# Four of eight block pairs by seven products, in alternation, in a hybrid decoder layer

## The chip, the core and the metric

The kernel runs on one core of a Trainium2 chip. The metric is the device time of one execution in microseconds (us); lower is better. The core's engines are TensorE (PE in the profile, its weight loads PEld), VectorE (DVE), ScalarE (ACT), GpSimd (POOL) and SyncE (SP). Here SP does nothing but issue the weight loads.

## What is computed

One decoder layer over 256 tokens of width 2048, all in float32: an input projection to 10240 columns, block attention over 8 heads and a short gated convolution side by side, their outputs gated by sigmoids, a mixing projection, cross-attention to 256 memory tokens, a squared-ReLU MLP of width 8192, and a final RMS norm. Cut to the lines that matter here:

```python
h = rms_norm(x, norm_mix)
q, k, v, cx, cb, cc, ga, gc = split_in_proj(h @ w_in)      # ga, gc: 2048 columns each
merged = sigmoid(ga) * y_attn + sigmoid(gc) * y_conv
x = x + merged @ w_mix_out
...
u = relu(rms_norm(x, norm_mlp) @ w_up)                     # 8192 columns
return rms_norm(x + (u * u) @ w_down, norm_final)
```

The two pieces that the change touches are `h @ w_in` for the gate columns, and `(u * u) @ w_down`.

## The kernel before

Every float32 product is made of three fp32r matmuls. A weight block arrives from memory as `raw`; ScalarE writes its rounded part `whi` (L71) and VectorE the remainder `wlo = raw - whi` (L72), 128 x 1024 at a time. The activations are split in the same way once. A product is then hi x hi + hi x lo + lo x hi, three 128x512 matmuls into one PSUM bank (lines 171 to 173 in the functions below).

Most projections go through `tok_group` or `feat_group`. The gate columns (three groups of 1024 columns: the second gate of the first half, and both gates of the second half) and the down projection go through `pair_group`, eleven calls in all. For the down projection the 8192 hidden features are taken in four rounds `g` of 2048. A round first makes its 2048 features by `feat_group` on `w_up` (four times 512), then calls `pair_group` twice (`jp` 0 and 1), each time for 1024 of the 2048 output columns.

`pair_group` works on 2 x 2 blocks: two halves of 128 tokens, two column blocks of 512, and eight pairs of 128-row contraction blocks. A pair is done in one of two ways:

- **direct**: four outputs of two products each, so 8 products or 24 matmuls. Of the weights it needs two splits of 128 x 1024 on each of ACT and DVE.
- **seven** (Strassen's scheme in Winograd's form): 7 products or 21 matmuls. DVE first makes four sums of weight blocks, `tsum` (L139 to L142, 128 x 512 each), which are split too. In all DVE has four sums, one split `olo` of 128 x 512 (L132) and three splits `wlo` of 128 x 1024. The sums of activations that it needs are made once for all calls, by `act_sums` into `hS` and `uS`.

The products of all pairs gather in eight PSUM banks, all that there are: six from the pool `mm` (`acc`) and two from `aux` (`aps`). Direct pairs add into four of them (numbers 2, 3, 4, 8), seven pairs into seven (1 to 7). When the last seven pair of a call is done, banks 1, 5, 6 and 7 are final, and ACT (L208) and DVE (L209 to L212) combine them into four blocks `p1, u4, u3, v`. When the last direct pair is done, banks 2, 3, 4 and 8 are final as well, and the call's consumer adds them: for the down projection `add_down` on DVE, L609 (the combined block into the residual `tok`) and L610 (the bank into `tok`), four of each per call; for the gates L466 on DVE and a sigmoid on ACT. The next call needs the same eight banks.

The order of the pairs in a call is a table, `MIXED` for the gates and `MIXED2` for the down projection, both with the same entries (pair, by seven or not). The order of instructions on each engine is not that of the code: a scheduler with a model of the chip's time sets it when the program is built. What limits how far one engine can run ahead are the buffers: four `raw`, five `whi`/`wlo`, two `tsum`, one `ohi`/`olo`. A load into a `raw` buffer is issued by SP, in order, as soon as ACT and DVE have read what was in it.

In the last call the final output block is halved (`fine`), and `last_sum` and `store` form the final norm. GpSimd helps with products by the norm's gain for the first half of the columns (L638).

## Time and profile before

| | |
|---|---|
| time, median of 3 runs | 1453.58 us (1453.27 to 1454.04) |
| the profiled execution | 1452.71 us, span of its instructions 1450.9 us |
| PE busy, share of the span | 1433.7 us, 99% |
| PEld (weight loads) | 1200.4 us, 83% |
| DVE | 1025.6 us, 71% |
| ACT | 752.2 us, 52% |
| POOL | 14.4 us, 1% |
| share of 16 DMA engines, mean rate | q1 59.7%, 195 GB/s |

The profile shows one execution. The span runs from its first to its last instruction. Busy time of PE is the union of matmul durations, which overlap each other, so 99% does not say that no time is lost between them; the distance between the starts of two matmuls does. The same holds of DVE: a duration in its rows reaches some hundredths of a microsecond into the next instruction, and the distance between two starts is what the instruction costs in a queue. Behind a row in brackets stands how long the engine sat idle before it, and what ended that.

### The profile page before, as it was taken

Reading aid. Unit: us, or ns where it says so; the run is one execution under the profiler, and the core shown is the slowest. Engines: PE = TensorE matmul, PEld = TensorE weight load, DVE = VectorE, ACT = ScalarE, POOL = GpSimd, SP = SyncE. Lnnn points to the kernel's source line nnn. Section 1 sums busy time; section 2 is a strip of 40 time slices with the busy share of each in tenths; the row PEclk is TensorE's granted clock in tenths of the full one; section 3 lists DMA queues with packets and bytes.
Section 4 is the critical chain, followed back from the end, with each engine's and each line's share of the span. In section 5 each row is a group of like instructions: output and inputs, shape, how many; then the busy total and the mean of one; then the engine's idle time right before and its main releaser. Section 6 shows DMA issues by size and latency. Waiting matters only on the chain.

```text
span 1450.9 us, 18458 instructions
## 1 busy us (share of the span) xinstructions
PE 1433.7 (99%) x6923; PEld 1200.4 (83%) x6923; DVE 1025.6 (71%) x1346; ACT 752.2 (52%) x999; POOL 14.4 (1%) x20
## 2 busy tenths in 40 slices
PE   8999999999999999999999999999999999999997
PEld 6888888888878888888888888888888888888875
DVE  6645555667679756654477689668896689866897
ACT  7644444445445545564565455445554555444553
POOL 0000000000000000000000000000000000000010
PEclk9999999999999999999999999999999999999999
DMA  9766555565656767755556566665665556655554
GB/s 320 231 192 185 169 176 172 170 193 189 198 169 196 233 221 266 237 186 186 162 174 183 181 194 211 192 196 170 199 217 190 188 161 212 219 192 183 179 176 145
DMA packets 122938, 283.39 MB, mean 195 GB/s; under 512 B 8928, under 2 KB 9696, under 8 KB 122464
## 3 DMA queue, kind: packets, MB, share of 16 engines
q1 hardware_dynamic: 119088, 273.58, 59.7%
q10 hardware_dynamic: 3760, 8.63, 1.8%
q8 instruction: 54, 0.88, 0.3%
q14 instruction: 36, 0.29, 0.1%
HBM read 280.08 MB, written 2.10 MB: 194 GB/s over the span
## 4 chain that ended last, share of the span: by engine, by line
PE 95%; DVE 2%; DMA 1%; ACT 0%; issue 0%; POOL 0%; SPq 0%; POOLq 0%; DVEq 0%; ACTq 0%
PE acc L83 15%; PE acc L108 13%; PE acc L110 13%; PE acc L109 13%; PE acc L84 8%; PE acc L172 6%; PE acc L173 6%; PE acc L171 6%; PE aps L171 4%; PE aps L172 4%; PE aps L173 4%; DMA raw<-in_w_in_dram 1%; PE acc L87 1%; PE aps L262 1%; DVE wlo L72 1%; PE acc L86 1%
## 5 line engine op out<-in xcount | busy, mean ns | idle before, releaser
L72 DVE TENSOR_TENSOR wlo<-raw,whi 128x1024 fp32r<-128x1024 f32 (+1 forms) x483 | 581.0, 1213 | 307.6 <-ACT whi L71 301.9
L71 ACT ACTIVATE whi<-raw 128x1024 fp32r<-128x1024 f32 (+1 forms) x483 | 500.5, 1050 | 401.2 <-PE acc L110 134.2
L83 PE MATMUL acc<-S,whi 128*128 128x512 f32 x960 | 341.6, 398 | 0.0
L108 PE MATMUL acc<-whi,S 128*128 128x512 f32 x816 | 315.5, 389 | 5.0 <-ACT whi L71 5.0
L110 PE MATMUL acc<-whi,S 128*128 128x512 f32 x816 | 317.3, 389 | 0.0
L109 PE MATMUL acc<-wlo,S 128*128 128x512 f32 x816 | 316.7, 388 | 0.0
L84 PE MATMUL acc<-S,wlo 128*128 128x256 f32 x960 | 269.6, 281 | 0.0
L83 PEld LDWEIGHTS acc<-S,whi 128*128 128x128 f32 x960 | 180.2, 188 | 41.1
L84 PEld LDWEIGHTS acc<-S,wlo 128*128 128x128 f32 x960 | 181.3, 189 | 3.1
L108 PEld LDWEIGHTS acc<-whi,S 128*128 128x128 f32 x816 | 153.6, 189 | 35.4 <-ACT whi L71 5.7
L109 PEld LDWEIGHTS acc<-wlo,S 128*128 128x128 f32 x816 | 153.7, 188 | 30.4
L110 PEld LDWEIGHTS acc<-whi,S 128*128 128x128 f32 x816 | 153.6, 188 | 30.2
L71 ACT ACTIVATE whi<-tsum 128x1024 fp32r<-128x1024 f32 x66 | 69.3, 1058 | 92.0 <-DVE tsum L142 41.8
L172 PE MATMUL acc<-wlo,S 128*128 128x512 f32 x255 | 99.6, 391 | 0.0
L173 PE MATMUL acc<-whi,S 128*128 128x512 f32 x255 | 99.1, 389 | 0.0
L172 PE MATMUL aps<-wlo,S 128*128 128x512 f32 (+1 forms) x253 | 98.3, 388 | 0.0
L173 PE MATMUL aps<-whi,S 128*128 128x512 f32 (+1 forms) x253 | 98.1, 388 | 0.0
L171 PE MATMUL aps<-whi,S 128*128 128x512 f32 (+1 forms) x253 | 95.4, 389 | 0.7 <-DVE tok L610 0.7
L171 PE MATMUL acc<-whi,S 128*128 128x512 f32 x255 | 92.5, 389 | 0.0
L72 DVE TENSOR_TENSOR wlo<-tsum,whi 128x1024 fp32r<-128x1024 f32 x66 | 79.1, 1219 | 15.1 <-ACT whi L71 14.2
L172 PEld LDWEIGHTS acc<-wlo,S 128*128 128x128 f32 x255 | 47.9, 188 | 10.9 <-DVE wlo L72 1.0
L171 PEld LDWEIGHTS aps<-whi,S 128*128 128x128 f32 x253 | 47.5, 188 | 11.3 <-DVE tok L610 1.1
(171 smaller groups left out, 1352.2 us busy)
## 6 DMA issues: line engine op xcount, KB each, us to landing
raw<-in_w_in_dram SPq DMA_DIRECT2D x156, 512.0 KB, 4.4
raw<-in_w_up_dram SPq DMA_DIRECT2D x128, 512.0 KB, 3.9
raw<-in_w_down_dram SPq DMA_DIRECT2D x128, 512.0 KB, 4.7
raw<-in_w_mix_out_dram SPq DMA_DIRECT2D x32, 512.0 KB, 5.0
raw<-in_w_attn_out_dram SPq DMA_DIRECT2D x16, 512.0 KB, 4.9
raw<-in_w_conv_out_dram SPq DMA_DIRECT2D x16, 512.0 KB, 4.5
raw<-in_wkv_x_dram SPq DMA_DIRECT2D x16, 512.0 KB, 4.4
raw<-in_wq_x_dram SPq DMA_DIRECT2D x8, 512.0 KB, 4.0
```

Source lines behind the costliest of these rows:

```text
L71: last_split[0] = nc.scalar.activation(hi[:, k:k + step, :], raw[:, k:k + step, :], AF.Copy)
L72: nc.vector.tensor_sub(lo[:, k:k + step, :], raw[:, k:k + step, :], hi[:, k:k + step, :].bitcast(F32))
L83: nc.tensor.matmul(ps, a, xs(k, 2), start=(k == 0), stop=False)
L84: nc.tensor.matmul(ps[:, S:], c, xs(k, 0), start=False, stop=False)
L86: nc.tensor.matmul(ps[:, S:], c, xs(k, 0), start=False, stop=False)
L87: nc.tensor.matmul(ps, a, xs(k, 2), start=(k == 0), stop=True)
L108: nc.tensor.matmul(ps, xh, wh, start=(k == 0), stop=False)
L109: nc.tensor.matmul(ps, xh, wl, start=False, stop=False)
L110: nc.tensor.matmul(ps, xl, wh, start=False, stop=(k == nk - 1))
L171: nc.tensor.matmul(ps, ah, bh, start=first, stop=False)
L172: nc.tensor.matmul(ps, ah, bl, start=False, stop=False)
L173: nc.tensor.matmul(ps, al, bh, start=False, stop=final)
```

## The change

The number of pairs that go by seven products rises from three to four, and the table of pairs becomes a strict alternation of seven and direct: pairs 0 to 3 by seven, 4 to 7 direct. Before, the three seven pairs alternated with three direct ones and two more direct pairs stood at the end. `NSEVEN` also sets how many activation sums are made for the gates; for the down projection `uS` and the condition in `ev_u` are widened to match.

```diff
-NSEVEN = 3
+NSEVEN = 4
...
-    MIXED = [(0, True), (3, False), (1, True), (4, False), (2, True), (5, False), (6, False), (7, False)]
-    MIXED2 = [(0, True), (3, False), (1, True), (4, False), (2, True), (5, False), (6, False), (7, False)]
+    MIXED = [(0, True), (4, False), (1, True), (5, False), (2, True), (6, False), (3, True), (7, False)]
+    MIXED2 = [(0, True), (4, False), (1, True), (5, False), (2, True), (6, False), (3, True), (7, False)]
...
-        uS = big.tile([P, 3, 2, 512], F32R, name="SS")
+        uS = big.tile([P, 4, 2, 512], F32R, name="SS")
...
-                    if k < 6:
+                    if k < 8:
                         act_sums(uS, k // 2, t)
```

Since a scheduler sets the order, the rows below show what it made of the table at three places. Numbers behind a name tell buffers apart.

DVE before, where the first call of round 0 ends and the second begins: from the last sums of the next call's first seven pair to the first split (`wlo_7236`) of that call's first direct pair.

```order
L141 TENSOR_TENSOR tsum_7182<-raw_7179,tsum_7181 128x512
L72 TENSOR_TENSOR wlo_7192<-raw_7179,whi_7191 128x1024
L142 TENSOR_TENSOR tsum_7182<-raw_7179,tsum_7182 128x512
L72 TENSOR_TENSOR wlo_7196<-tsum_7181,whi_7195 128x1024
L72 TENSOR_TENSOR wlo_7200<-tsum_7182,whi_7199 128x1024
L139 TENSOR_TENSOR tsum_7272<-raw_7268 128x512
L610 SCALAR_TENSOR_TENSOR tok_4397<-acc_6862,q3_6020,tok_4397 128x512
L140 TENSOR_TENSOR tsum_7272<-raw_7270,raw_7268 128x512
L610 SCALAR_TENSOR_TENSOR tok_4397<-acc_6866,q3_6020,tok_4397 128x512
L72 TENSOR_TENSOR wlo_7236<-raw_7231,whi_7235 128x1024
```

The row ahead of these is `wlo_7134`, the last split of the first call; L209 to L212 and all four L609 stand further ahead, among the splits of the direct pairs at the call's end.

DVE now, at the same place, up to the split `wlo_7297` that answers to `wlo_7236`. Ahead of these rows stand `wlo_7195` (the last split of the first call), an L609 and the split `olo_7249` (L132).

```order
L72 TENSOR_TENSOR wlo_7253<-raw_7240,whi_7252 128x1024
L209 TENSOR_TENSOR blk_7222<-acc_6928,blk_7222 128x512
L72 TENSOR_TENSOR wlo_7257<-tsum_7242,whi_7256 128x1024
L72 TENSOR_TENSOR wlo_7261<-tsum_7243,whi_7260 128x1024
L210 TENSOR_TENSOR blk_7223<-acc_6924,blk_7222 128x512
L211 TENSOR_TENSOR blk_7223<-acc_6920,blk_7222 128x512
L139 TENSOR_TENSOR tsum_7333<-raw_7329 128x512
L610 SCALAR_TENSOR_TENSOR tok_4440<-acc_6912,q3_6063,tok_4440 128x512
L140 TENSOR_TENSOR tsum_7333<-raw_7331,raw_7329 128x512
L212 TENSOR_TENSOR blk_7224<-acc_6920,blk_7223 128x512
L609 SCALAR_TENSOR_TENSOR tok_4440<-blk_7223,q3_6063,tok_4440 128x512 x2
L72 TENSOR_TENSOR wlo_7297<-raw_7292,whi_7296 128x1024
```

L209 to L212 and three of the four L609 have moved from ahead of the last split of the first call to between it and the first direct split of the second. The other three rounds read the same.

PE before, in the same stretch, up to the first matmul that needs `wlo_7236`:

```order
L171 MATMUL acc_7207<-whi_7235,S2_6029 128x512
L171 MATMUL acc_7211<-whi_7235,S2_6029 128x512
L171 MATMUL acc_7219<-whi_7195,SS_6030 128x512
L172 MATMUL acc_7219<-wlo_7196,SS_6030 128x512
L173 MATMUL acc_7219<-whi_7195,SS_6030 128x512
L171 MATMUL acc_7223<-whi_7199,SS_6030 128x512
L172 MATMUL acc_7223<-wlo_7200,SS_6030 128x512
L173 MATMUL acc_7223<-whi_7199,SS_6030 128x512
L171 MATMUL acc_7203<-ohi_7278,S2_6029 128x512
L172 MATMUL acc_7207<-wlo_7236,S2_6029 128x512
```

PE now, up to the first matmul that needs `wlo_7297`:

```order
L171 MATMUL acc_7276<-whi_7256,SS_6073 128x512
L172 MATMUL acc_7276<-wlo_7257,SS_6073 128x512
L173 MATMUL acc_7276<-whi_7256,SS_6073 128x512
L171 MATMUL acc_7264<-ohi_7339,S2_6072 128x512
L171 MATMUL acc_7280<-whi_7256,SS_6073 128x512
L172 MATMUL acc_7280<-wlo_7257,SS_6073 128x512
L173 MATMUL acc_7280<-whi_7256,SS_6073 128x512
L171 MATMUL acc_7276<-whi_7347,SS_6073 128x512
L171 MATMUL acc_7280<-whi_7347,SS_6073 128x512
L172 MATMUL acc_7268<-wlo_7297,S2_6072 128x512
```

From the first matmul on the last split of the first call (`wlo_7195`) to this last row there are 30 matmuls; ohi_7339 and whi_7347, of the call's second seven pair, are pulled ahead of the direct pair that precedes it.

DVE at the end of the program, from the last split on: before,

```order
L72 TENSOR_TENSOR wlo_11970<-raw_11963,whi_11969 128x1024
L610 SCALAR_TENSOR_TENSOR tok_4397<-acc_11698,q3_6020,tok_4397 128x512
L610 SCALAR_TENSOR_TENSOR tok_4397<-acc_11702,q3_6020,tok_4397 128x512
L638 TENSOR_TENSOR tok_4397<-tok_4397,S3_6022 128x512
L642 TENSOR_REDUCE pre0_6025<-ssf_6024 128x1
L610 SCALAR_TENSOR_TENSOR tok_4397<-aps_11718,q3_6020,tok_4397 128x512
```

and now:

```order
L72 TENSOR_TENSOR wlo_12129<-raw_12122,whi_12128 128x1024
L209 TENSOR_TENSOR blk_12163<-acc_11862,blk_12163 128x512
L210 TENSOR_TENSOR blk_12164<-acc_11858,blk_12163 128x512
L211 TENSOR_TENSOR blk_12164<-acc_11854,blk_12163 128x512
L212 TENSOR_TENSOR blk_12165<-acc_11854,blk_12164 128x512
L609 SCALAR_TENSOR_TENSOR tok_4440<-blk_12164,q3_6063,tok_4440 128x512 x2
L609 SCALAR_TENSOR_TENSOR tok_4440<-blk_12165,q3_6063,tok_4440 128x256
L610 SCALAR_TENSOR_TENSOR tok_4440<-acc_11846,q3_6063,tok_4440 128x512
```

L209 to L212 and three L609 now stand behind the last split; before, they stood ahead of it.

## Rows read from the trace of the kernel before

**Rows 1.** The page's first part: busy us, share of the span, instructions.

```profile
PE 1433.7 (99%) x6923; PEld 1200.4 (83%) x6923; DVE 1025.6 (71%) x1346; ACT 752.2 (52%) x999; POOL 14.4 (1%) x20
```

**Rows 2.** The page's chain that ended last, by engine.

```profile
PE 95%; DVE 2%; DMA 1%; ACT 0%; issue 0%; POOL 0%; SPq 0%; POOLq 0%; DVEq 0%; ACTq 0%
```

**Rows 3.** Waits of PE: who waited for whom, us in total, times, longest.

```profile
PE acc L108 <- ACT whi L71: 5.0, 2, 4.6
PE aps L171 <- DVE tok L610: 0.7, 1, 0.7
```

**Rows 4.** Timeline of PE: start, us, instruction; a first gate call.

```profile
337.94 0.39 PE L171 MATMUL acc<-whi,SS 128*128 128x512 f32 x1
338.16 0.39 PE L172 MATMUL acc<-wlo,SS 128*128 128x512 f32 x1
338.39 0.39 PE L173 MATMUL acc<-whi,SS 128*128 128x512 f32 x1
338.62 0.39 PE L172 MATMUL acc<-wlo,S 128*128 128x512 f32 x1
```

**Rows 5.** Groups of DVE instructions by line: count, then busy us, mean ns.

```profile
L132 DVE TENSOR_TENSOR olo<-raw,ohi 128x512 fp32r<-128x512 f32 x33 | 23.7, 717 | 0.0
L209 DVE TENSOR_TENSOR blk<-acc,blk 128x512 f32<-128x512 f32 x11 | 7.5, 682 | 0.0
```

**Rows 6.** Busy time by stretch; round 0's two down calls, then round 1's `w_up`.

```profile
833.42:916.90 83.48, 83.48 (x366) 68.35 (x365) 75.35 (x90) 43.99 (x49) 0.00 (x0) 1.00 0.64 203
930.00:1005.00 75.00, 75.00 (x427) 65.00 (x425) 51.58 (x73) 36.01 (x50) 0.00 (x0) 1.00 0.60 190
```

**Rows 7.** Timeline of DVE between round 0's two down calls.

```profile
865.52 0.74 DVE L609 SCALAR_TENSOR_TENSOR tok<-blk,q,tok 128x512 f32<-128x512 f32 x1
866.18 0.68 DVE L139 TENSOR_TENSOR tsum<-raw 128x512 f32<-128x512 f32 x1
866.78 0.74 DVE L609 SCALAR_TENSOR_TENSOR tok<-blk,q,tok 128x512 f32<-128x512 f32 x1
...
869.31 1.22 DVE L72 TENSOR_TENSOR wlo<-raw,whi 128x1024 fp32r<-128x1024 f32 x1
870.45 0.69 DVE L141 TENSOR_TENSOR tsum<-raw,tsum 128x512 f32<-128x512 f32 x1
...
877.67 0.69 DVE L140 TENSOR_TENSOR tsum<-raw 128x512 f32<-128x512 f32 x1 [1.00 <-DMA raw<-in_w_down_dram]
878.28 0.75 DVE L610 SCALAR_TENSOR_TENSOR tok<-acc,q,tok 128x512 f32<-128x512 f32 x1
878.94 1.22 DVE L72 TENSOR_TENSOR wlo<-raw,whi 128x1024 fp32r<-128x1024 f32 x1
```

**Rows 8.** Timeline of PE: first matmuls on wlo_7134 and on wlo_7236.

```profile
873.02 0.39 PE L172 MATMUL acc<-wlo,S 128*128 128x512 f32 x1
...
880.21 0.50 PE L172 MATMUL acc<-wlo,S 128*128 128x512 f32 x1
```

**Rows 9.** Timelines, DVE's last split of a direct pair and PE's first use.

```profile
849.81 1.22 DVE L72 TENSOR_TENSOR wlo<-raw,whi 128x1024 fp32r<-128x1024 f32 x1
852.37 0.39 PE L172 MATMUL acc<-wlo,S 128*128 128x512 f32 x1
...
897.38 2.35 DVE L72 TENSOR_TENSOR wlo<-raw,whi 128x1024 fp32r<-128x1024 f32 x2
902.86 0.39 PE L172 MATMUL acc<-wlo,S 128*128 128x512 f32 x1
```

**Rows 10.** Timeline of DVE, and loads of `w_down`: count, KB, us to landing.

```profile
845.73 0.69 DVE L139 TENSOR_TENSOR tsum<-raw 128x512 f32<-128x512 f32 x1 [3.19 <-DMA raw<-in_w_down_dram]
raw<-in_w_down_dram SPq DMA_DIRECT2D x128, 512.0 KB, 4.7
```

**Rows 11.** Timelines of PE, DVE and POOL at the program's end.

```profile
1440.45 0.28 PE L173 MATMUL acc<-whi,S 128*128 128x256 f32 x1
...
1440.40 0.47 DVE L610 SCALAR_TENSOR_TENSOR tok<-aps,q,tok 128x256 f32<-128x256 f32 x1
1440.80 0.15 DVE L617 TENSOR_TENSOR rf<-ssf,pre 128x1 f32<-128x1 f32 x1
...
1442.26 0.47 DVE L610 SCALAR_TENSOR_TENSOR tok<-acc,q,tok 128x256 f32<-128x256 f32 x1
1442.65 0.74 DVE L627 SCALAR_TENSOR_TENSOR tok<-tok,rf,S 128x512 f32<-128x512 f32 x1
...
1444.40 0.57 POOL L618 TENSOR_TENSOR rf<-rf,mhalf 128x1 f32<-128x1 f32 x1 [0.69 <-DVE rf L617]
```

## The prediction

> **What bounds the kernel now.** I read the page's first part, then the chain, PE's waits, and then the stretches of the two down calls one by one. PE is busy 99% of the span [rows 1] and makes 95% of the chain that ended last [rows 2], and in the whole program it is seen to wait for others only a few times, once for 4.6 us and otherwise for 0.7 us or less [rows 3]. So TensorE sets the time. What a matmul costs is not its duration of 0.39 us but the step to the next start: 338.16 to 338.39 to 338.62 is 0.227 us, with no gap where seven pair and direct pair meet [rows 4]. The granted clock is 1.00, the 2.4 GHz level, throughout the down calls [rows 6].
>
> DVE is idle 29% of the span, but that is an average. In the 83.48 us of round 0's two down calls it works 75.35 us, 90%; in the `w_up` stage between, 51.58 of 75 us [rows 6]. The reserve in the stage that the change loads is 8.1 us, and it is not free: DVE sits waiting there for weights, once for 3.19 us [rows 10]. And PE's cover is thin at one place. Where the first call passes into the second, DVE ends the split `wlo_7236` at 878.94 + 1.22 = 880.16 [rows 7] and PE uses it at 880.21 [rows 8]: a lead of 0.05 us. Nothing stalled in this execution, but nothing was left.
>
> **What the change removes.** One `olo` split comes with each seven pair and one L209 with each call, 33 and 11 [rows 5]: three seven pairs in eleven calls. A fourth turns 24 matmuls into 21 in each call, 33 matmuls in all, at 0.227 us each [rows 4]: **-7.5 us** on the engine that is the chain. Of TensorE the Trainium skill (TensorE: Matmul & The Clock Gate, Back-to-back issue gap) gives some 131 ns as the sustained distance at 512 columns; the trace shows 227, and the measurement decides. By the page's figure, as an estimate, the saving would be 4.3 us and the forecast 3.2 us later.
>
> **What it adds to DVE.** In a full queue a 128x512 sum or split costs 0.60 us (866.18 to 866.78), an L609 or L610 0.66 (865.52 to 866.18), a 128x1024 split 1.14 (869.31 to 870.45) [rows 7]. A seven pair is then 5 x 0.60 + 3 x 1.14 = 6.42 us of DVE, a direct pair 2.28: **+4.1 us per call**. A down call's DVE work, with 4 x 0.60 for L209 to L212 and 8 x 0.66 for L609 and L610, goes from 3 x 6.42 + 5 x 2.28 + 7.7 = 38.4 us to 42.5; PE's goes from 183 x 0.227 = 41.5 to 180 x 0.227 = 40.9. Before, DVE had 3 us to spare per call; now it is 1.6 us over. The Trainium skill (Perfetto Trace Analysis, Identifying the Most-Contended Engine) says to judge TensorE by its weight loads rather than its matmuls, and to relieve the engine that is fullest; in these two calls weight loads take 68.35 of 83.48 us, 82%, against DVE's 90%, so by that rule the change helps the wrong engine.
>
> ACT gains 1.5 splits of 1024 a call and is busy 43.99 of 83.48 us [rows 6], so it covers them. The fourth activation sum (four small sums and a split) falls into `w_up`, where DVE is idle a third of the time, and into the start for the gates, where it is likewise hidden; if not, some 2 us five times, which I put into no term since nothing waits on it for tens of microseconds. Loads are the same in number and size.
>
> **Where it lands: between the two down calls.** Before, the call ended with three direct pairs, 3 x 24 x 0.227 = 16 us of PE for 6.8 us of DVE. In that slack DVE did L209 to L212 and the L609. Now the last seven pair is second to last, so its banks are final one pair, 5.4 us, before the end, and this work moves behind the last split. I check the reckoning on before: from the end of `wlo_7134` (869.31 + 1.22 = 870.53) to that of `wlo_7236` (880.16) DVE took 9.63 us, 8.28 of work by the prices above and the rest around the 1.00 us wait for a load [rows 7]. PE used the two at 873.02 and 880.21, 7.19 us apart [rows 8]. The lead was 2.49 us, and 2.49 + 7.19 - 9.63 = 0.05: it closes.
>
> Now the same sum for the changed order. From the end of `wlo_7195` to that of `wlo_7297` DVE has 14 instructions: four splits of 1024 (4.56), three L609 and one L610 (2.64), seven of 0.60 (L132, L209 to L212, L139, L140; 4.20), together 11.4 us. PE has 30 matmuls there, 6.8 us. DVE's lead at `wlo_7195` I take from five direct pairs that follow a seven pair in round 0, from 851.03 to 852.37 = 1.34 us (the first of them) to 899.73 to 902.86 = 3.13 us (the last) [rows 9]; the others are 1.86, 1.43 and 2.10, and the mean is 2.0. So PE waits 11.4 - 6.8 - 2.0 = 2.6 us. The next two splits are late as well: `wlo_7301` comes 1.74 us later (L141, split) where PE has 6 matmuls, 1.36 us: 0.4 more; `wlo_7344` 2.4 us later (L132, L609, split) for 8 matmuls, 1.8 us: 0.6 more. A wait for a load is likely too, since a seven pair holds its `raw` buffers longer and a load lands 4.7 us after its issue [rows 10]: 0 to the 1.0 us of before [rows 7], I take 0.5. That is **4.1 us per round**, 16.2 in four. Bounds: the lead of 3.13 and no load wait, 2.4 a round, 9.6; the lead of 1.34 and 1.0, 5.2 a round, 20.9. After that the alternation gives DVE 8.7 us of work for 10.2 us of PE in each two pairs, so it regains a lead and I count nothing until the end of the second call, where the evacuation meets `w_up` with its idle DVE.
>
> Between the two gate calls of the second half the same happens, with L466 (0.60 each) in place of L609 and L610: 16 instructions, 4 x 1.14 + 12 x 0.60 = 11.8 us against 37 matmuls, 8.4 us, less the lead of 2.0: **1.4 us** (0.2 to 3.0). The first gate call is followed by `tok_group`, which asks little of DVE: nothing.
>
> **The end of the program.** Before, the last L610 starts at 1442.26, 1.69 us after PE's last matmul gave way (1440.45 + 0.12) [rows 11]. Now DVE has after its last split four combinations (2.4), three L609 (1.7), three full and one half L610 (2.4), the halves and the L638 (2.4): 8.9 us until that last L610, while PE needs 2.3 us from that split's first use to its end. With a lead of 2.0 it starts 4.6 us after PE, 2.9 later than before. Both L617 now stand behind it, with L627 and L631 for the first half behind them (before, L617 came at 1440.80 and L627 at 1442.65, under cover [rows 11]): 0.7 more. **+3.6 us** (1.5 to 6).
>
> **The sum** against the profiled execution: 1452.71 - 7.5 + 16.2 + 1.4 + 3.6 = 1466.4 us. The runs' median is 0.87 us above that execution, so **1467 us**; the bounds of the terms give +3.8 to +22.4, 1457 to 1476.
>
> **Rivals.** A: the cover holds. If DVE enters each boundary with some 5 us more lead than I take, all 7.5 us come through: 1446 us. For it speaks that PE hardly ever waited, and the lead in front of some splits is above 4 us; against it, 0.05 us at the place itself, and more DVE work than PE work in a call. It ends faster. Chance 0.12. B: DVE becomes the bound but drops its idle time. The two calls of a round then take 75.35 + 8.28 = 83.6 us instead of 83.48, the gates keep their 2 us, and only the end is paid: +2.0, 1455.6 us, no change. For it: a late engine makes its loads early for the one that waits. Against: loads are issued when DVE has read the buffer, so a late DVE makes late loads. Chance 0.14. C: DVE keeps its 8.1 us of idle time per round, because the four `raw` buffers and not the boundary set the pace: 83.6 + 8.1 - 83.5 = 8.2 us a round, 33 in all, with the end and the gates' saving 1488 us. It decides from the point where each alternation, not just each boundary, shows DVE waiting for loads. Chance 0.09. That the change does not do what it says is ruled out by the order: the fourth sum and split are there, and 21 matmuls where 24 were.
>
> **Chances.** The forecast has 0.65. About 0.2%, 2.9 us, is what a measurement of this kernel can tell from no change. Faster is A, 0.12; the same is B, 0.14; slower is the forecast and C, 0.74. The range runs from 1449 us, between A and B, to 1478, above the bounds and short of C.
>
> **What would show it.** PE waiting for DVE (L72, or L610 through a bank) by 2 to 5 us in each round some 40 us after its down calls begin, with DVE above 95% busy in the two calls; gaps in PE's starts nowhere else but between the gates and at the end; PE's count down by 33. If those gaps are missing, the lead was the wrong term. If DVE waits for loads in each pair, it is C. If the last L610 starts within 2 us of PE's end, the end was.

## The result and the profile after

The changed kernel is slower: 1487.97 us (1486.0 to 1491.39) against 1453.42 (1453.22 to 1454.04) for the kernel before on the same chip, a ratio of 1.0234 [1.0215, 1.0252], the brackets holding the 95% interval. Of each run below the time, its range and its ratio to the kernel before, measured beside it, stand in the same form. The sign of the forecast was right; its size was not: 1467 us was forecast, with a range to 1478.

The page of the changed kernel gives TensorE's and DVE's busy time, then the chain of work that ended last, by engine and by line, and then the group of the first weight sum, L139: the busy time of the group, the mean duration of one, and the idle time in front of them with what ended it.

```profile
PE 1440.1 (97%) x6890; PEld 1195.3 (80%) x6890; DVE 1078.8 (73%) x1439; ACT 772.3 (52%) x1026; POOL 19.3 (1%) x20
...
PE 69%; DVE 13%; DMA 12%; issue 3%; ACT 1%; POOL 0%; SPq 0%; POOLq 0%; DVEq 0%; ACTq 0%
...
L139 DVE TENSOR_TENSOR tsum<-raw 128x512 f32<-128x512 f32 x44 | 31.5, 716 | 53.0 <-DMA raw<-in_w_down_dram 41.1
```

In the chain before, PE made 95%, DVE 2% and DMA 1% [rows 2]; now DMA has 12%. The 33 matmuls are gone (6923 to 6890), but DVE waits 53.0 us in front of L139, 41.1 of them for a load of `w_down`. Before, that was 23.8 and 16.8 us for 33 of them.

PE's waits, longest first in total (us, times, longest), were one of 4.6 us and little else before [rows 3]. Now:

```profile
PE acc L172 <- DVE wlo L72: 9.1, 11, 2.1
PE acc L171 <- DVE blk L210: 5.4, 4, 1.4
PE acc L171 <- DVE tok L610: 5.3, 4, 1.5
PE acc L171 <- ACT whi L71: 4.8, 4, 1.2
PE acc L108 <- ACT whi L71: 4.6, 1, 4.6
PE acc L171 <- ACT ohi L131: 1.8, 3, 0.9
```

Four at L210, four at L610 and four at `whi`: one for each round. The four rounds' down calls, as stretches of the span (duration, then busy time of PE, PEld, DVE, ACT and POOL with the count of instructions, then granted clock, DMA share, GB/s):

```profile
833.99:924.25 90.26, 84.03 (x360) 66.77 (x359) 79.44 (x96) 47.16 (x53) 0.00 (x0) 1.00 0.57 185
1014.90:1105.70 90.80, 84.33 (x361) 66.69 (x360) 79.40 (x96) 47.02 (x53) 0.00 (x0) 1.00 0.59 185
1196.30:1288.30 92.00, 85.47 (x361) 68.01 (x360) 79.56 (x96) 47.09 (x53) 0.00 (x0) 0.98 0.57 182
1378.90:1472.00 93.10, 86.57 (x367) 68.85 (x365) 81.37 (x97) 46.36 (x58) 6.09 (x4) 0.96 0.46 147
```

Round 0 took 83.48 us before [rows 6]. The table shows where the 35.5 us between the two spans (1450.9 and 1486.4) went. A stretch runs from the start of its first matmul to that of its last.

| stretch | before | after | difference |
|---|---|---|---|
| down calls, round 0 | 83.50 | 90.27 | +6.8 |
| round 1 | 83.14 | 90.79 | +7.7 |
| round 2 | 83.11 | 91.92 | +8.8 |
| round 3 | 85.27 | 93.05 | +7.8 |
| the three gate calls | 41.47 + 85.37 | 41.37 + 84.40 | -1.1 |
| last matmul's start to the end of the span | 10.5 | 14.5 | +4.0 |
| start to the first gate call | 332.9 | 334.5 | +1.6 |

The last line is not the change: that start lies between 332.7 and 335.4 us in the runs below, whatever the table of pairs. The loss is in the down calls, and in each round alike. A round of the changed kernel is 360 matmuls, 359 steps of 0.227 us or 81.5 us; the rest, 8.8 us in round 0, is lost time.

The longer end is seen in the start of PE's last matmul, of the last L610 and of the last L617 (before: 1440.45, 1442.26 and, under cover, 1440.80 [rows 11]):

```profile
1471.95 0.28 PE L173 MATMUL acc<-whi,S 128*128 128x256 f32 x1
...
1475.89 0.48 DVE L610 SCALAR_TENSOR_TENSOR tok<-acc,q,tok 128x256 f32<-128x256 f32 x1
...
1477.01 0.16 DVE L617 TENSOR_TENSOR rf<-ssf,pre 128x1 f32<-128x1 f32 x1 [0.51 <-ACT junk L636]
```

DVE's instructions in round 0 (start, duration, in brackets the idle time ahead and what ended it). The four L139 are the first sums of the last two seven pairs of the first call and of the first two of the second; the two L72 are the splits of the first call's last direct pair:

```profile
845.03 0.69 DVE L139 TENSOR_TENSOR tsum<-raw 128x512 f32<-128x512 f32 x1 [2.39 <-DMA raw<-in_w_down_dram]
...
850.25 0.69 DVE L132 TENSOR_TENSOR olo<-raw,ohi 128x512 fp32r<-128x512 f32 x1
...
857.85 0.69 DVE L139 TENSOR_TENSOR tsum<-raw 128x512 f32<-128x512 f32 x1 [2.91 <-DMA raw<-in_w_down_dram]
...
861.93 0.69 DVE L132 TENSOR_TENSOR olo<-raw,ohi 128x512 fp32r<-128x512 f32 x1
...
868.19 0.69 DVE L139 TENSOR_TENSOR tsum<-raw 128x512 f32<-128x512 f32 x1 [1.56 <-DMA raw<-in_w_down_dram]
869.36 0.69 DVE L140 TENSOR_TENSOR tsum<-raw 128x512 f32<-128x512 f32 x1 [0.48 <-DMA raw<-in_w_down_dram]
...
870.57 1.22 DVE L72 TENSOR_TENSOR wlo<-raw,whi 128x1024 fp32r<-128x1024 f32 x1
...
872.31 1.22 DVE L72 TENSOR_TENSOR wlo<-raw,whi 128x1024 fp32r<-128x1024 f32 x1
...
880.78 0.69 DVE L139 TENSOR_TENSOR tsum<-raw 128x512 f32<-128x512 f32 x1 [0.79 <-DMA raw<-in_w_down_dram]
```

Each of the four L139 waits for its load. In strict alternation a seven pair's weights come into the two buffers that the seven pair before it has used. That pair holds the first of them from L139 to the end of L132 (845.03 to 850.94, and 857.85 to 862.62), and only then does the reload begin: 6.9 us until the next L139, then 5.6. Three turns take 880.78 - 845.03 = 35.75 us, 11.9 each, while PE needs 45 matmuls, 10.2 us, for a seven and a direct pair. DVE falls behind by 1.7 us a turn until PE waits. Before, the last seven pair of round 0's first call waited so too (3.19 us [rows 10]), but three direct pairs followed it, and the next L139, at 866.18 [rows 7], waited for nothing.

PE's stall comes where the prediction put it, at the passage, and it meets an engine without a lead:

```profile
871.84 0.50 PE L172 MATMUL acc<-wlo,S 128*128 128x512 f32 x1 [1.20 <-DVE wlo L72]
...
874.27 0.39 PE L172 MATMUL acc<-wlo,S 128*128 128x512 f32 x1
```

The first row uses the first split of the last direct pair, which DVE ends at 870.57 + 1.22 = 871.79, behind two sums that have waited 1.56 and 0.48 us for loads; it starts 1.36 us later than a step of 0.227 would have it. The second row uses the call's last split. Five more such delays, of 0.4 to 1.5 us, follow at 879.45, 882.19, 885.55, 889.99 and 894.77; the six make 7.2 us of the 8.8. Of the signs that the prediction named, the waits at the passage came and PE's count is down by 33; DVE above 95% busy did not come. It is 88% busy in the two calls, 79.44 of 90.26 us.

### The profile page after: what moved, and what is told of

It reads as the page before. It is cut to its first block, busy times and chain, and to the rows that moved or that the text cites. A ratio compares the mean times of both kernels' runs of the same rounds, so it can differ in the third digit from the quotient of the medians.

```text
span 1486.4 us, 18542 instructions
## 1 busy us (share of the span) xinstructions
PE 1440.1 (97%) x6890; PEld 1195.3 (80%) x6890; DVE 1078.8 (73%) x1439; ACT 772.3 (52%) x1026; POOL 19.3 (1%) x20
## 4 chain that ended last, share of the span: by engine, by line
PE 69%; DVE 13%; DMA 12%; issue 3%; ACT 1%; POOL 0%; SPq 0%; POOLq 0%; DVEq 0%; ACTq 0%
PE acc L83 14%; PE acc L108 11%; PE acc L110 11%; PE acc L109 11%; DMA raw<-in_w_down_dram 8%; PE acc L84 7%; DVE wlo L72 6%; DMA raw<-in_w_in_dram 4%; PE acc L172 3%; PE acc L173 2%; PE acc L171 2%; PE aps L173 1%; PE aps L172 1%; PE aps L171 1%; DVE tsum L141 1%
## 5 line engine op out<-in xcount | busy, mean ns | idle before, releaser
L72 DVE TENSOR_TENSOR wlo<-raw,whi 128x1024 fp32r<-128x1024 f32 (+1 forms) x472 | 568.6, 1215 | 264.5 <-ACT whi L71 258.4
L108 PE MATMUL acc<-whi,S 128*128 128x512 f32 x816 | 315.2, 390 | 4.7 <-ACT whi L71 4.6
L110 PE MATMUL acc<-whi,S 128*128 128x512 f32 x816 | 317.9, 390 | 0.0
L109 PE MATMUL acc<-wlo,S 128*128 128x512 f32 x816 | 317.3, 389 | 0.0
L83 PEld LDWEIGHTS acc<-S,whi 128*128 128x128 f32 x960 | 180.0, 188 | 40.9
L108 PEld LDWEIGHTS acc<-whi,S 128*128 128x128 f32 x816 | 153.9, 189 | 35.4 <-ACT whi L71 5.4
L109 PEld LDWEIGHTS acc<-wlo,S 128*128 128x128 f32 x816 | 153.9, 189 | 30.3
L72 DVE TENSOR_TENSOR wlo<-tsum,whi 128x1024 fp32r<-128x1024 f32 x88 | 105.8, 1221 | 14.1 <-ACT whi L71 13.0
L172 PE MATMUL acc<-wlo,S 128*128 128x512 f32 (+1 forms) x222 | 89.8, 405 | 9.1 <-DVE wlo L72 9.1
L173 PE MATMUL acc<-whi,S 128*128 128x512 f32 (+1 forms) x222 | 87.7, 395 | 0.0
L172 PE MATMUL aps<-wlo,S 128*128 128x512 f32 x220 | 85.5, 389 | 0.0
L173 PE MATMUL aps<-whi,S 128*128 128x512 f32 x220 | 83.2, 388 | 0.0
L171 PE MATMUL aps<-whi,S 128*128 128x512 f32 (+1 forms) x220 | 82.2, 389 | 0.0
L171 PE MATMUL acc<-whi,SS 128*128 128x512 f32 x176 | 66.7, 405 | 15.8 <-DVE blk L210 5.4
L171 PE MATMUL acc<-whi,S 128*128 128x512 f32 x222 | 79.9, 394 | 0.0
L139 DVE TENSOR_TENSOR tsum<-raw 128x512 f32<-128x512 f32 x44 | 31.5, 716 | 53.0 <-DMA raw<-in_w_down_dram 41.1
```

The source lines that it names most:

```text
L72: nc.vector.tensor_sub(lo[:, k:k + step, :], raw[:, k:k + step, :], hi[:, k:k + step, :].bitcast(F32))
L83: nc.tensor.matmul(ps, a, xs(k, 2), start=(k == 0), stop=False)
L108: nc.tensor.matmul(ps, xh, wh, start=(k == 0), stop=False)
L109: nc.tensor.matmul(ps, xh, wl, start=False, stop=False)
L110: nc.tensor.matmul(ps, xl, wh, start=False, stop=(k == nk - 1))
L139: nc.vector.tensor_sub(ta[:, 0, :], r1_[:, 1, :], r1_[:, 0, :])
```

## Experiments

Round durations are those of the table above (first to last matmul start); "lost" is a round's duration less its matmuls at 0.227 us.

**Where the seven pairs stand, or how many there are.** Two theories at first: PLACE (the last seven pair stands too near the call's end, so the evacuation meets the next call) and WORK (a fourth seven pair is more work for DVE than there is time).

`e_late3`: three seven pairs as before, moved to the end (both tables).

```diff
-    MIXED2 = [(0, True), (3, False), (1, True), (4, False), (2, True), (5, False), (6, False), (7, False)]
+    MIXED2 = [(0, True), (3, False), (4, False), (1, True), (5, False), (6, False), (2, True), (7, False)]
```

> Three seven pairs as before, but spread so that the last one stands second to last in each call (seven, direct, direct, seven, direct, direct, seven, direct). TensorE and VectorE have exactly the work of the kernel before. Theory PLACE (the loss comes from where the last seven pair stands, because the combination of the banks then falls behind the last split and the next call waits for splits and for free banks): 5 to 8 us at each of the four passages between down calls and about 4 us at the end, 1475 to 1488 us. Theory WORK (VectorE has more work per call than TensorE, wherever it stands): 1453 to 1457 us.

1461.65 us (1460.95 to 1463.97), 1.0055 [1.0040, 1.0070]. Between the two: with the work of before the place costs 8 us, a quarter of the loss (and DVE idles 32.7 us ahead of L139 instead of 23.8).

`e_early4`: four seven pairs, with two direct pairs at the end (both tables).

```diff
-    MIXED2 = [(0, True), (4, False), (1, True), (5, False), (2, True), (6, False), (3, True), (7, False)]
+    MIXED2 = [(0, True), (4, False), (1, True), (2, True), (5, False), (3, True), (6, False), (7, False)]
```

> Four seven pairs, with two direct pairs at the end of each call (seven, direct, seven, seven, direct, seven, direct, direct). Work on every engine as in the changed kernel. PLACE: the passages cost less than half of what they cost in the changed kernel and the end is as before, 1453 to 1466 us. WORK: as the changed kernel, 1483 to 1492 us, only the stalls stand elsewhere in the calls.

1466.98 us (1463.63 to 1473.18), 1.0093 [1.0067, 1.0120]: again between, 21 us better than the changed kernel, 13.5 worse than before. Its rounds take 86.9 to 88.3 us, and PE's waits, apart from the 5.9 us at L108 outside the pairs, are of another kind:

```profile
PE acc L171 <- ACT ohi L131: 5.7, 4, 1.9
PE acc L172 <- DVE wlo L72: 5.2, 6, 2.0
```

Here two seven pairs stand next to each other, and there is one `ohi` buffer: the second pair's `ohi` must wait for the first's. DVE waits less for loads, 13.8 us ahead of L139 in the whole program. ScalarE sat idle 17.3 us ahead of L131 in the whole program until a matmul had read that buffer. So both runs fell between the two theories, and neither theory alone gives either number.

**Which calls.** `e_gates` has the changed table in the gate calls alone, `e_down` in the down calls alone.

```diff
# e_gates, against the kernel before
-NSEVEN = 3
+NSEVEN = 4
...
+    MIXED = [(0, True), (4, False), (1, True), (5, False), (2, True), (6, False), (3, True), (7, False)]
```

> The change in the three gate calls alone; the down calls as before. Both theories: TensorE saves 9 matmuls (2.0 us), of which the changed kernel's trace showed 1.1 us left after one wait between the gates, and lost 1.6 us in the first stage, where the fourth activation sum now stands: 1453 to 1455 us.

1454.75 us (1451.69 to 1457.51), 1.0001 [0.9991, 1.0011]: as expected, nothing.

```diff
# e_down, against the changed kernel
-NSEVEN = 4
+NSEVEN = 3
...
+    MIXED = [(0, True), (3, False), (1, True), (4, False), (2, True), (5, False), (6, False), (7, False)]
```

> The change in the eight down calls alone; the gates as before. Both theories: all but about 0.5 us of the loss stays, 1485 to 1490 us.

1490.14 us (1487.46 to 1493.87), 1.0250 [1.0229, 1.0270]: the whole loss is in the down calls. `e_tail3` puts the program's last call alone back (`MIXED3` is the table of before).

```diff
-            pair_group(w_down, jp * 1024, g * KG, KG, parts_of(uT), uS, MIXED2, ev_d, last and jp == 1)
+            pair_group(w_down, jp * 1024, g * KG, KG, parts_of(uT), uS, MIXED3 if last and jp else MIXED2, ev_d, last and jp == 1)
```

> The changed kernel with only the last call of the program (second down call of round 3) in the order of before, three seven pairs and three direct ones at its end. The last call loses its saving of 3 matmuls (+0.7 us). If the end term is what the prediction made it (3.6 us) or the trace (4.0 us), and the last round's own stalls of 2 to 4 us in that call go too: 1481 to 1485 us. If the end is set by something else (the norm), no change: 1487 to 1489.

1484.68 us (1483.39 to 1485.17), 1.0209 [1.0195, 1.0223], 3.3 us less than the changed kernel. Round 3 shrinks from 93.05 to 90.68 us and the end from 14.5 to 12.2. Why the end isn't back at 10.5 with the old table in its place was not settled.

**The evacuation.** Now three theories: EVACUATION, the prediction's own (L209 to L212 and L609 stand between the splits of two calls), WORK as above, and LOADS, which is rival C (the four `raw` buffers set the pace). `e_bare0` leaves them out (with L208) in the first down call of rounds 0 to 2.

```diff
...
+        if bare:
+            for q, h, j in ((2, 0, 0), (3, 0, 1), (4, 1, 0), (8, 1, 1)):
+                evac(h, j, bank[q], None)
+            return
...
-        nc.vector.scalar_tensor_tensor(t, u, r, t, op0=ALU.mult, op1=ALU.add)
+        if u is not None:
+            nc.vector.scalar_tensor_tensor(t, u, r, t, op0=ALU.mult, op1=ALU.add)
...
-            pair_group(w_down, jp * 1024, g * KG, KG, parts_of(uT), uS, MIXED2, ev_d, last and jp == 1)
+            pair_group(w_down, jp * 1024, g * KG, KG, parts_of(uT), uS, MIXED2, ev_d, last and jp == 1, bare=jp == 0 and not last)
```

> The changed kernel, but in the first down call of rounds 0 to 2 the combination is left out: no L208 to L212 and no L609, so VectorE has 8 instructions (5.0 us) less there and four banks are free at once. The output misses those terms. Theory EVACUATION (at the passage the combination stands in VectorE's queue ahead of the next call's splits and holds its banks): each of the three passages falls from 8 to 10 us to 1 to 4, 1464 to 1474 us. Theory LOADS (four weight buffers set the pace): at most 1.5 us per passage, 1483 to 1488 us. Theory WORK (VectorE's total): 5 us in each of three rounds, 1470 to 1476 us.

1487.95 us (1485.08 to 1491.2), 1.0231 [1.0211, 1.0250]: no gain at all from eight DVE instructions less, some 5 us, at each of three passages. DVE's idle time ahead of L139 rose from 53.0 to 75.8 us in the whole program, so its time went into waiting, here in round 0:

```profile
846.90 0.69 DVE L139 TENSOR_TENSOR tsum<-raw 128x512 f32<-128x512 f32 x1 [3.42 <-DMA raw<-in_w_down_dram]
859.92 0.69 DVE L139 TENSOR_TENSOR tsum<-raw 128x512 f32<-128x512 f32 x1 [3.10 <-DMA raw<-in_w_down_dram]
...
883.67 0.69 DVE L139 TENSOR_TENSOR tsum<-raw 128x512 f32<-128x512 f32 x1 [3.93 <-DMA raw<-in_w_down_dram]
898.43 0.69 DVE L139 TENSOR_TENSOR tsum<-raw 128x512 f32<-128x512 f32 x1 [3.34 <-DMA raw<-in_w_down_dram]
910.37 0.69 DVE L139 TENSOR_TENSOR tsum<-raw 128x512 f32<-128x512 f32 x1 [3.16 <-DMA raw<-in_w_down_dram]
```

That is rival C's sign: each of the six seven pairs whose first sum falls into these two calls waits for its load (the one not shown, at 870.40, for 1.70 us). PE sees it through other instructions, since what waits behind an L139 in DVE's queue waits with it. In this run PE waits 10.7 us for L615 (the L610 of the other kernels), which frees a bank and stands behind such an L139; in round 0 that of 883.67. `e_bare1` leaves the same out in the second call of the rounds.

```diff
-            pair_group(w_down, jp * 1024, g * KG, KG, parts_of(uT), uS, MIXED2, ev_d, last and jp == 1)
+            pair_group(w_down, jp * 1024, g * KG, KG, parts_of(uT), uS, MIXED2, ev_d, last and jp == 1, bare=jp == 1 and not last)
```

> The same left out in the second down call of rounds 0 to 2, which is followed by the up projection. Just as much work of VectorE and ScalarE is missing as in the run before. EVACUATION: the passage between the two calls is untouched, so 0 to 3 us in all, 1484 to 1488 us. WORK: as the run before, 1470 to 1476 us.

1487.97 us (1487.32 to 1490.62), 1.0234 [1.0217, 1.0251]: nothing either. That is what EVACUATION and LOADS both expected, and WORK falls.

**The loads.** `e_raw5` gives the changed kernel a fifth `raw` buffer (`pT`, needed early only, shares a buffer to make room).

```diff
-    wraw = ctx.enter_context(tc.tile_pool(name="wraw", bufs=4))
+    wraw = ctx.enter_context(tc.tile_pool(name="wraw", bufs=5))
...
-        tag = {"s": "ta", "xsum": "ta", "junk": "ta", "rsw": "tc", "y": "tc"}.get(name, name)
+        tag = {"s": "ta", "xsum": "ta", "junk": "ta", "rsw": "tc", "y": "tc", "pT": "tc"}.get(name, name)
```

> The changed kernel with five instead of four weight buffers (raw), made room for by letting the transposed attention weights share a scratch buffer. The order of instructions at the passage between the down calls is nearly the same. LOADS: VectorE's waits for loads, 9 us in each round of the changed kernel, largely go, and with them half or more of the loss, 1460 to 1474 us. EVACUATION: only the wait ahead of the first call's last direct pair goes, some 1.4 us a round, 1480 to 1488 us.

1470.87 us (1469.52 to 1472.87), 1.0114 [1.0097, 1.0131]: 17 us back, half of the loss, with no work taken away. Nor is the rate at which memory delivers the limit: with as many bytes to load, the two calls moved 203 GB/s before [rows 6] and 185 in the changed kernel. A gap that repeats on an engine can mean that too few buffers are there for the next tile, says the Trainium skill (Perfetto Trace Analysis, Optimization Strategy), of the engine that should be saturated. The gap ahead of L139 is such a one, though on DVE, which was taken for the busy one. DVE's idle time ahead of L139 falls from 53.0 to 26.3 us:

```profile
L139 DVE TENSOR_TENSOR tsum<-raw 128x512 f32<-128x512 f32 x44 | 30.3, 688 | 26.3 <-DMA raw<-in_w_down_dram 19.3 <-DMA raw<-in_w_in_dram 7.0
```

Of the 17 us that are left, 4 are the program's end, which is as long as with four buffers (14.6 us from the last matmul's start). Is the rest the evacuation, which the loads had hidden? `e_bare0_r5` is `e_bare0` with five buffers.

> The changed kernel with five raw buffers and, in the first down call of rounds 0 to 2, without the combination L208 to L212 and without the four L609, so 8 DVE instructions, some 5 us of DVE, are missing at each of three passages. With four buffers leaving them out gained nothing (1487.95 against 1487.97 us), with five buffers alone the time was 1470.87. If loads hid the evacuation and it is what is left once a fifth buffer relieves them (the passage as the prediction had it, second in line), each of the three passages gains 2 to 4 us: 1458 to 1465 us. If the rest of the loss still is the loads, it stays at 1468 to 1472 and DVE is seen to wait at L139 in most pairs of the first call.

1470.53 us (1468.79 to 1472.09), 1.0113 [1.0099, 1.0127]: again no gain. DVE's idle time ahead of L139 is 43.3 us, against 26.3 with the evacuation left in. At the passage of round 0, DVE, with less to do, comes earlier and waits longer:

```profile
874.06 0.69 DVE L139 TENSOR_TENSOR tsum<-raw 128x512 f32<-128x512 f32 x1 [3.02 <-DMA raw<-in_w_down_dram]
875.25 0.69 DVE L140 TENSOR_TENSOR tsum<-raw 128x512 f32<-128x512 f32 x1 [0.50 <-DMA raw<-in_w_down_dram]
875.86 0.74 DVE L615 SCALAR_TENSOR_TENSOR tok<-acc,q,tok 128x512 f32<-128x512 f32 x1
...
876.66 0.50 PE L171 MATMUL acc<-whi,SS 128*128 128x512 f32 x1 [2.52 <-DVE tok L615]
```

The L615 at 875.86 is the addition that frees a bank; PE starts 0.06 us after its end (875.86 + 0.74 = 876.60). So either of two things might do: the load, or DVE's work. To part them, `e_keep` (changed kernel, four buffers) takes the loads away and leaves all the work: in the down calls of rounds 0 to 2 only the first pair loads, and the other seven pairs use its weights again.

```diff
-            r = [load_row(w, kr0 + k + i, c0) for i in range(2)]
+            if not keep or pair == order[0][0]:
+                r = [load_row(w, kr0 + k + i, c0) for i in range(2)]
...
-            pair_group(w_down, jp * 1024, g * KG, KG, parts_of(uT), uS, MIXED2, ev_d, last and jp == 1)
+            pair_group(w_down, jp * 1024, g * KG, KG, parts_of(uT), uS, MIXED2, ev_d, last and jp == 1, keep=not last)
```

> The changed kernel, but in the down calls of rounds 0 to 2 only the first pair of each call loads its two raw blocks; the other seven pairs use these two again (so the weights of seven of eight pairs are left out there). All sums, splits, products and evacuations stay, in nearly the same order on DVE. Four raw buffers as before. LOADS (the waits for reloads of raw are the whole loss in these rounds): a round's two calls fall from 90.3 to 91.9 us to 82 to 83, three rounds gain 25 to 28: 1460 to 1463 us. PASSAGE (DVE's work at the passage stalls PE by itself, hidden so far behind the loads): 2 to 4 us a round stay, at the first direct split behind the passage and at the banks: 84 to 86.5 us a round, 1466 to 1474 us. WORK (DVE's and PE's work alone set the pace, loads never did): no gain, 1484 to 1490.

1462.67 us (1461.26 to 1463.16), 1.0058 [1.0045, 1.0072]: 25 us back, from three rounds of four, and the rounds take 82.5 us instead of 90.3 to 91.9. Two of them as stretches (columns as above):

```profile
835.82:918.40 82.58, 82.40 (x361) 67.28 (x360) 79.21 (x96) 46.84 (x53) 0.00 (x0) 1.00 0.12 38
1008.95:1091.50 82.55, 82.38 (x361) 67.23 (x360) 79.17 (x96) 46.68 (x53) 0.00 (x0) 1.00 0.12 38
```

DVE is 96% busy in them, with the same 96 instructions as in the changed kernel, and the rounds are shorter than the 83.1 to 83.5 us of before. What is left over the matmuls is 1.0 us a round. This is the prediction's passage with its DVE work and without loads (L610 is the L609 of the other kernels):

```profile
867.25 2.37 DVE L72 TENSOR_TENSOR wlo<-raw,whi 128x1024 fp32r<-128x1024 f32 x2 [0.94 <-ACT whi L71]
...
878.46 1.41 DVE L610 SCALAR_TENSOR_TENSOR tok<-blk,q,tok 128x512 f32<-128x512 f32 x2
879.78 1.22 DVE L72 TENSOR_TENSOR wlo<-raw,whi 128x1024 fp32r<-128x1024 f32 x1
```

```profile
874.36 0.39 PE L172 MATMUL acc<-wlo,S 128*128 128x512 f32 x1
...
881.05 0.50 PE L172 MATMUL acc<-wlo,S 128*128 128x512 f32 x1
```

The last split of the first call ends at 867.25 + 2.37 = 869.62, and PE first uses it at 874.36: a lead of 4.74 us. The split `wlo` of the next call's first direct pair ends at 881.00 and is used at 881.05. DVE took 11.4 us between the two ends, PE 6.7 between the two uses: the reckoning of the prediction to a tenth. Only the lead was not 2.0 but 4.7, and that just covers it. PE is then late once in the round, by 0.3 us at 885.19. The loads don't make DVE's instructions themselves slower: a split followed by a sum takes 1.13 us from start to start here (879.78 to 880.91) and 1.13 in the changed kernel (884.58 to 885.71).

`e_keep_bare0` takes the first down call's evacuation away too.

```diff
# against e_keep; the lines under `if bare:` and `if u is not None:` as in e_bare0
-            pair_group(w_down, jp * 1024, g * KG, KG, parts_of(uT), uS, MIXED2, ev_d, last and jp == 1, keep=not last)
+            pair_group(w_down, jp * 1024, g * KG, KG, parts_of(uT), uS, MIXED2, ev_d, last and jp == 1, keep=not last, bare=jp == 0 and not last)
```

> As e_keep, and the combination L208 to L212 and the four L609 of the first down call of rounds 0 to 2 left out too. LOADS: nothing left to gain, equal to e_keep within 1 us. PASSAGE: 2 to 4 us a round less than e_keep, 6 to 12 in all, to 1460 to 1463 us.

1461.89 us (1459.43 to 1463.45), 1.0053 [1.0038, 1.0068]: 0.8 us below `e_keep`, which the two ranges don't tell apart, with rounds of 81.9 instead of 82.5. Without load waits the work that is left out is worth 0.6 us a round. The theory of the loads holds; that of the passage as a cause of its own falls. The passage is where PE loses its time, since DVE comes there without a lead.

The control is `e_before_r5`, the kernel before with the same two lines changed.

> The kernel before with five raw buffers instead of four, nothing else. If four buffers are too few only for a strict alternation, and the three direct pairs at the end of a call let the loads catch up, PE has nothing to gain (its stalls in the four rounds sum to 3.4 us, most of it in the last): 1450.5 to 1454.5 us. If the fifth buffer helps whatever the order, for a reason that has to do with other stages, the gain seen in the changed kernel (17 us) should show here too: 1435 to 1447.

1449.17 us (1448.36 to 1450.64), 0.9966 [0.9956, 0.9977]: faster than expected. The last round falls from 85.27 to 83.38 us, the gates of the second half from 85.37 to 84.03. So loads cost the kernel before something as well, where an average of 99% busy hid it, but 4.8 us and not 17.

**Places where the change gains.** `e_where` keeps the change where a stage follows that leaves DVE time, or nothing does: first and third gate call, second down call of rounds 0 to 2.

```diff
-                pair_group(w_in, c0, 0, KD, hx, hS, MIXED, ev_g)
+                pair_group(w_in, c0, 0, KD, hx, hS, MIXED3 if jp and not i else MIXED, ev_g)
...
-            pair_group(w_down, jp * 1024, g * KG, KG, parts_of(uT), uS, MIXED2, ev_d, last and jp == 1)
+            pair_group(w_down, jp * 1024, g * KG, KG, parts_of(uT), uS, MIXED2 if jp and not last else MIXED3, ev_d, last and jp == 1)
```

(`MIXED3` is the table of before.)

> Four seven pairs only in the calls that are followed by a stage with idle VectorE: the first and third gate call and the second down call of rounds 0 to 2; the other six as before. PLACE: 15 matmuls (3.4 us) saved and at most 1 us lost in each call, 1449 to 1454 us. WORK: VectorE is over in each of these calls by about 1.6 us and what it waits for loads, 1460 to 1475 us.

1452.31 us (1448.16 to 1454.24), 0.9983 [0.9972, 0.9994]: a little faster than before. The changed rounds take 82.5, 83.2 and 83.2 us, although DVE idles 34.6 us ahead of L139, more than before. So with four buffers, one alternating call in a round, with `w_up` behind it, is covered, and these waits for loads cost no time there. `e_where_r5` adds the fifth buffer.

> Four seven pairs only in the first and third gate calls and in the second down call of rounds 0 to 2, the other six calls as before, now with five raw buffers. With four buffers: 1452.31. Where the passage behind each of these calls has slack (a w_up or tok stage follows), only loads inside the call can stall PE, and the trace showed 0.3 to 1 us per round: 1451 to 1453 us if the loads are relieved, 1452 to 1454 if they weren't what is left.

1446.19 us (1446.13 to 1446.93), 0.9947 [0.9935, 0.9960], five us below the expectation, which had taken from one round's trace that little was left to gain. `e_best` has four seven pairs in all three gate calls, the rest as there.

> Five raw buffers, four seven pairs in all three gate calls and in the second down call of rounds 0 to 2; the first down calls and the last call as before. Beside the variant with the second gate call as before (1446.19 us) three matmuls less, 0.68 us; with five buffers the two gate calls of the second half took 82.8 us with four seven pairs each and 83.4 with three in the first of them. 1445 to 1446.5 us if that passage has slack with five buffers; 1447 to 1449 if it stalls there.

1445.35 us (1444.73 to 1445.94), 0.9941 [0.9930, 0.9953]: the fastest of all, 8 us below before and 43 below the change as it was made. In a round PE's busy time fills the stretch, and PE waits for no pair any more:

```profile
830.96:913.50 82.54, 82.54 (x364) 67.99 (x363) 75.27 (x91) 45.53 (x51) 0.00 (x0) 1.00 0.62 204
```

```profile
PE acc L108 <- ACT whi L71: 4.9, 2, 4.7
PE acc L108 <- ACT SS L249: 0.3, 1, 0.3
```

Against `e_before_r5` it saves 3.8 us; its 18 matmuls less (three in each of six calls) are 18 x 0.227 = 4.1. There the seven products give almost all that they promise.

## Why the prediction was right or wrong

- **TensorE sets the time, and 33 matmuls are worth 7.5 us.** Right. Counts and steps came out so, and in `e_best` the saving arrives.
- **DVE's work per call, 42.5 us against PE's 40.9.** The prices were right, the conclusion was not: in `e_keep` DVE does it all and PE loses 1.0 us a round. The budget charged each call with its whole evacuation, but part of the second call's ends up in `w_up`, as the same text said further on. In the two calls DVE ran 96 instructions instead of 90, where the budget has twelve more, and its busy time rose from 75.35 [rows 6] to 79.4 us, by 4.1 and not 8.3.
- **The passage, 2.6 us and 0.4 and 0.6.** Here is the step that failed: the lead. The work of 11.4 us (of 15 instructions in the prediction's own list, though it counts 14) and PE's 6.8 were right, as `e_keep` shows. The lead of 2.0 us was an average of five pairs in a kernel where loads already held DVE back at 845.73 [rows 9, 10]; it was taken as a property of the work. Without load waits it is 4.7 us, and of the 2.6, 0.4 and 0.6 us of stalls 0.3 us is left. With the changed kernel's load waits, it is 0.7: `wlo_7195` ends at 872.31 + 1.22 = 873.53 and is used at 874.27.
- **The load wait, 0.5 us a round at the passage.** The term that was mis-sized, and the cause of the short lead. A round loses 7 to 9 us more than before, and taking the loads away gives back 7.8 (90.27 to 82.49), 8.3 and 9.4. The prediction said that a seven pair holds its buffers longer and that a late DVE makes late loads, and still priced this at one row's 1.00 us, a wait from an order in which three direct pairs let the loads catch up. It did not compare the turn of a buffer, held and reloaded, with PE's time for a turn. That could have been done with its own prices: a seven pair's blocks are read by five instructions of 0.60 us and a split of 1.14, and the direct pair's two splits of 1.14 stand among them, 6.4 us; with 4.7 for the load [rows 10] a turn is 11.1 us, against 10.2 of PE. That is an estimate and near the 11.9 measured in part by luck: in the trace a buffer is held 4.8 to 5.9 us and comes back after 5.6 to 6.9.
- **Banks and single buffers.** Left out of the sum. PE's waits for L210, L610 (banks) and `whi` appear in every round, 15.5 us in all; they are the form that DVE's lateness takes, not a cause of their own, for they go when the loads go: in `e_keep` they stand in the fourth round alone, which still loads.
- **The gates, +1.4 less the saving.** Near enough: neutral, as `e_gates` says. Their stretch in the second half took 84.4 to 87.2 us in different runs with four seven pairs and four buffers, and 82.8 with five.
- **The end, +3.6.** Right in size, +4.0. The last L610 started 1.69 us after PE gave way [rows 11] and now 3.8 (PE's last start 1471.95 + 0.12, L610 at 1475.89), so 2.1 later where 2.9 was expected; the rest, 1.9, is L617, which now starts last at 1477.01, and what stands behind it.
- **Rival C, 1488 us.** It gave the time, within 0.1 us, and its sign is in the trace: DVE kept its idle time (83.48 - 75.35 = 8.1 us in round 0 before [rows 6], 90.26 - 79.44 = 10.8 after) and waits for loads at the seven pairs up to the passage, though behind it at only one of two (905.90, 1.06 us). It was given 0.09. Its price of 8.2 us a round rests on that idle time alone, so part of the agreement is luck: the idle time grew, and DVE's work grew less than it took. What spoke for C was in the text: "loads are issued when DVE has read the buffer, so a late DVE makes late loads". It was used against B and not for C.
- **Rivals A and B** assumed a lead and loads that follow. With the loads taken away, A's 5 us of lead is there. Neither it nor B comes true with four buffers.
- **The rule of the fullest engine.** By the Trainium skill (Perfetto Trace Analysis, Identifying the Most-Contended Engine) the engine with the highest occupancy is optimized first, so the change helps the wrong engine. The time agrees, but in `e_bare0` DVE is relieved and nothing is gained, and `e_keep` has DVE at 96% and PE with 1.0 us lost; the measured limit is a wait, which busy shares don't show.

What stays open: how much of the loss in rounds 2 and 3 is the lower clock (last section), and why five buffers give back a half and not all. In `e_raw5`, DVE still waits 26.3 us for loads at L139, and in round 0's two calls the median load takes 5.8 us from issue to landing instead of 5.1, which would take back part of the gain; no run tests that, and six buffers were not tried.

## What to carry to other kernels

Before loading more work onto one side of a ring of buffers (buffers that are filled and read in turn), work out a buffer's turn: the time from its first read to its last, plus the time from there to the next first read, and compare it with the bottleneck engine's time for the same turn; in this kernel an order that groups easy pieces at the end let the ring recover, and two strictly alternating calls in a row didn't. A lead that is read from a trace belongs to that trace's waits, and can't be carried into one with other waits. If leaving work out of a busy engine gains nothing, see whether its idle time grew instead, and take away the thing it then waits for, with the work left in.

## What the hardware showed that was not expected

**TensorE's clock fell twice behind stretches with stalls.** Before, the granted clock stood at 1.00, the 2.4 GHz level, until PE was done. In the changed kernel it fell to 0.50, the 1.2 GHz level, twice within the down calls, from 1249.62 to 1253.03 us and from 1430.52 to 1437.35. The rows of the two stretches, and of the 9 us ahead of the first (columns as above):

```profile
1249.60:1253.00 3.40, 3.40 (x10) 2.62 (x9) 3.40 (x5) 0.00 (x0) 0.00 (x0) 0.50 0.58 181
1430.50:1437.30 6.80, 5.60 (x14) 3.83 (x13) 6.80 (x9) 1.10 (x2) 0.46 (x1) 0.50 0.37 105
1240.00:1249.00 9.00, 4.95 (x18) 2.77 (x16) 7.92 (x11) 4.07 (x5) 0.00 (x0) 1.00 0.40 130
```

In those 9 us PE was busy for 4.95; in the 12.5 us ahead of the second stretch, from 1418.0, for 9.30. In round 0 it was busy for 6.68 of the 10.5 us from 875.0, and the clock stayed at 1.00. In the slow stretch the step from matmul to matmul is 0.43 us:

```profile
1250.36 0.63 PE L173 MATMUL acc<-whi,S 128*128 128x512 f32 x1
1250.79 0.63 PE L171 MATMUL acc<-whi,S 128*128 128x512 f32 x1
1251.22 0.63 PE L172 MATMUL acc<-wlo,S 128*128 128x512 f32 x1
```

With 10 and 14 matmuls at 0.2 us more, that is at most 2.0 and 2.8 us, in the two rounds that lost most. It can't be the source of the loss, for round 0 lost 8.8 us at a full clock. That the stalls bring it about is argued from the order in time; no run here shows it by itself.

**Loads come in bursts.** In round 0 of the changed kernel, in 40 slices of 2.25 us (GB/s moved):

```profile
GB/s 0 100 317 251 237 31 13 251 279 279 111 22 231 284 351 51 0 189 209 240 291 2 0 109 264 273 126 160 0 240 381 273 46 198 300 266 184 226 270 329
```

Slices of 250 to 350 stand beside slices of 0 to 50. The kernel before is no different, with slices from 0 to 363 in its two calls; that buffers come free in bursts would explain it and was not tested. So a mean of 185 GB/s says little about whether a load is in time: those of one seven pair took 5.6 to 6.9 us from the last read of the buffer to the next first read, while the median from issue to landing in these calls is 5.1.
